# Hybrid decoder trunk on one core: longer load times in the planner's count, the MLP weight sums moved from GpSimd to VectorE, and earlier adding loads for the second MLP product

## The chip, the cores and the metric

The kernel runs on one core of a Trainium2 chip. The metric is the device time of one execution in microseconds (us). TensorE (PE) does the matrix products, VectorE (DVE) and ScalarE (ACT) the elementwise work, GpSimd (POOL) a few sums and the adding loads, and SyncE (SP) issues nearly all DMA transfers.

## The reference

Two decoder layers over x of 1024 tokens by 1024 channels, all in float32. Each layer has a mixer and an MLP, each behind an RMS norm whose output is scaled and shifted by vectors computed from a conditioning vector c.

```python
c_act = silu(c)
for layer in range(2):
    mod = c_act @ ada_w[layer] + ada_b[layer]          # 6 vectors of 1024
    h = rmsnorm(x) * (1 + sc_m) + sh_m
    y = even_mixer(h) if layer == 0 else odd_mixer(h)  # recurrences, retention, gated delta rule
    x = x + gt_m * y
    h = rmsnorm(x) * (1 + sc_f) + sh_f
    x = x + gt_f * (square(relu(h @ w1)) @ w2)         # w1 1024 x 4096, w2 4096 x 1024
out = rmsnorm(x)
```

## The kernel before

**Products in three parts.** A float32 operand is split into a rounded high part (one ACT instruction) and a remainder (one DVE subtraction), and each product is three matmuls of 128x128 by 128x512: high by high, high by low, low by high. The splits of weights go to tiles named `w` (6 slots), those of activations to the general pool `heap` (73 slots of 128x512).

**The MLPs.** Both MLP products use a Winograd form with 7 block products instead of 8. It needs sums of weight blocks. For the first product ("up", `up_factor`) a step s brings two rows of weights in two tiles `raw` (4 slots) and a tile `pad` (4 slots). A block sum x = a21 + a22 is made by an adding load: SP loads a21, then GpSimd issues a DMA that adds a22 on top (`dma_add`). Two more sums are made by an elementwise addition on GpSimd (`G.tensor_tensor`): x + a11 ahead of kind P6, and P2 + x ahead of kind P3. There are 16 steps of 7 kinds in each layer, 112 items of 12 matmuls each. The results go to the DRAM buffer `h_spill`, 7 tiles a step.

The second product ("down", `down_factor`, the last loop of `mlp`) has two groups of 8 steps; a group runs through the kinds P1 P2 P6 P7 P4 P5 P3 with 8 items of 12 matmuls each, 56 items a group and 112 in all. Item n loads its activations six items ahead (`load_h`). The five weight blocks of a step come by `load_block`, at item numbers relative to the group's first item that `W_LOADS` lists: `a11` from 8 items before the group, `a12` from item 0, `x` at 1, 3, ... 15, `a21` at 10, 12, ... 24, and `a22` from 24. `x` and `a21` are a load on SP with an adding load behind it on GpSimd. Two sums per step are made on GpSimd: a11 + x ahead of P6 (items 16 to 23) and a12 + a11 ahead of P7 (items 24 to 31). When the eight items of a kind are done, DVE drains four PSUM banks; after P1 and P6 the drained values go to tiles `blk` (`shared`), and P2 goes on accumulating in the banks of P1. `X_LOADS` brings the residual x back from `x_spill`. `last_adds` adds `shared` to it in the last group.

**The modulation vectors.** A column of `mod` costs one load of 128x1024 into a `raw` tile and one multiply-and-sum on DVE (`ada_unit`). Most are made beside the first mixer; the last 16 of layer 1 are made in the down product of layer 0, one at every item n with n % 4 == 2.

**The order.** Nothing is ordered by hand. Every instruction is recorded with an estimated duration, and `place()` plays the program through once at build time: of the instructions whose inputs it counts as ready, each engine takes the one of highest priority. The order that comes out is fixed for each engine and each DMA issuer, and the engines run it strictly in that order. A load counts as landed by

```python
dma_free = max(dma_free, now) + op.bytes / 380.0
op.end = dma_free + 2000.0
```

in nanoseconds, adding loads with twice their bytes. Weight work has the highest priority (`bias(-2 * BIG)`), the drains come next, and the matmuls follow program order.

Of the kernel before, what the change touches and what calls it, by code (L numbers as in the profile page):

```python
# [16 lines left out]
ALU = mybir.AluOpType  # L17
# [140 lines left out]
class Recorder:  # L158
# [59 lines left out]
    def place(self):  # L218
        free = {p: list(range(t.n)) for p, t in self.pools.items()}
        front = {}  # L220
        for p, d in self.unplaced.items():
            front[p] = sorted(d)
        for op in self.ops:
            op.npred, op.ready, op.start = len(op.preds), 0.0, None
            for p in op.preds:
                p.succ.append(op)
        queue = {p: deque(self.fifo[p]) for p in FIFO}
        waiting = {e: [] for e in ENGINES}
        avail = {e: [] for e in ENGINES}
        engine_free = {e: 0.0 for e in ENGINES}  # L230
        dma_free = port_free = 0.0
        events = [(0.0, 0, 0)]
        frees = []
        tick = 0
        for op in self.ops:
            if not op.npred:
                heapq.heappush(waiting[op.eng], (0.0, op.prio, op.seq))
        order = []

        def placeable(op, now):  # L240
            need = {}
            for b in op.bufs:
                if b.busy > now:
                    return False
                if b.pool is not None and b.slot is None:
                    need[b.pool] = need.get(b.pool, 0) + 1
            for b in op.bufs:
                if b.pool in FIFO and b.slot is None and b is not queue[b.pool][0]:
                    return False
            for p, n in need.items():  # L250
                lead = front[p]
                while lead and not self.unplaced[p][lead[0]]:
                    lead.pop(0)
                keep = 0 if op.group <= lead[0] else self.reserve.get(p, 0)
                if len(free[p]) < n + keep:
                    return False
            return True

        while len(order) < len(self.ops):
            if not events:  # L260
                raise RuntimeError("no instruction can be placed")
            now = events[0][0]
            while events and events[0][0] <= now:
                heapq.heappop(events)
            while frees and frees[0][0] <= now:
                _, _, b = heapq.heappop(frees)
                free[b.pool].append(b.slot)
            for e in ENGINES:
                w = waiting[e]
                while w and w[0][0] <= now:  # L270
                    _, prio, seq = heapq.heappop(w)
                    heapq.heappush(avail[e], (prio, seq))
                if engine_free[e] > now:
                    continue
                skipped = []
                chosen = None
                while avail[e]:
                    item = heapq.heappop(avail[e])
                    op = self.ops[item[1]]
                    if placeable(op, now):  # L280
                        chosen = op
                        break
                    skipped.append(item)
                for item in skipped:
                    heapq.heappush(avail[e], item)
                if chosen is None:
                    if w:
                        heapq.heappush(events, (w[0][0], tick, 0))
                        tick += 1
                    continue  # L290
                op = chosen
                for b in op.bufs:
                    if b.pool is not None and b.slot is None:
                        b.slot = free[b.pool].pop(0)
                        self.unplaced[b.pool][b.group] -= 1
                        if b.pool in FIFO:
                            queue[b.pool].popleft()
                op.start = max(now, port_free) if op.port else now
                engine_free[e] = op.start + op.dur
                if op.port:  # L300
                    port_free = engine_free[e]
                if e in ("DVE", "ACT"):
                    for b in op.bufs:
                        if b.pool in ("psum", "dps"):
                            b.busy = engine_free[e]
                if op.bytes:
                    dma_free = max(dma_free, now) + op.bytes / 380.0
                    op.end = dma_free + 2000.0
                else:
                    op.end = engine_free[e]  # L310
                heapq.heappush(events, (engine_free[e], tick, 0))
                tick += 1
                order.append(op)
                for s in op.succ:
                    kind = s.preds[op]
                    t = op.start if kind is None else op.end + LATENCY.get((op.eng, s.eng), 150)
                    s.ready = max(s.ready, t)
                    s.npred -= 1
                    if not s.npred:
                        heapq.heappush(waiting[s.eng], (s.ready, s.prio, s.seq))  # L320
                        heapq.heappush(events, (max(s.ready, now), tick, 0))
                        tick += 1
                for b in op.bufs:
                    b.left -= 1
                    b.last = max(getattr(b, "last", 0.0), op.end)
                    if not b.left and b.pool is not None:
                        heapq.heappush(frees, (b.last, tick, b))
                        heapq.heappush(events, (max(b.last, now), tick, 0))
                        tick += 1
        self.order = order  # L330
        return max(op.end for op in order)
# [77 lines left out]
class Tensor:  # L409
# [17 lines left out]
    def transpose(self, o, i, ident):  # L427
# [14 lines left out]
PN = {k: n for n, k in enumerate(UP_ORDER)}  # L442

X_LOADS = {i + n * m: (f, k + m) for i, n, f, k in ((2, 2, 0, 0), (23, 2, 1, 4), (32, 1, 0, 4), (40, 1, 1, 0)) for m in range(4)}
W_LOADS = {(i + n * j, name): j for i, n, name in ((-8, 1, "a11"), (0, 1, "a12"), (1, 2, "x"), (10, 2, "a21"), (24, 1, "a22"))
           for j in range(GRP)}

AHEAD = 4
# [7 lines left out]
def trunk_kernel(ctx, tc, xT, pos, ada0, ada, cols, hsc, lw_a, lw_x, w_ev, w_evo, w_od, w_odg,  # L456
# [142 lines left out]
    def split(dst_hi, dst_lo, src, after=(), eng=V):  # L599
        act(dst_hi, src, AF.Copy, after)  # L600
        eng.tensor_tensor(dst_lo, src, dst_hi.bitcast(F32), ALU.subtract)


    units = []
    loads = {}
# [33 lines left out]
    def up_factor(l, s, kind, pw):  # L639

        a11, a12 = w_1[l, 2 * s][:, 0:HT], w_1[l, 2 * s][:, HT:D]
        a21, a22 = w_1[l, 2 * s + 1][:, 0:HT], w_1[l, 2 * s + 1][:, HT:D]

        def load():

            r = rec.tile("raw")
            dma(r, w_1[l, 2 * s])
            pw["P1"], pw["P2"] = r[:, 0:HT], r[:, HT:D]
            pw["x"] = padded()[:, 0:HT]
            dma(pw["x"], a21)  # L650
            dma_add(pw["x"], a22)
            r = rec.tile("raw")
            dma(r, w_1[l, 2 * s + 1])
            pw["P7"], pw["P4"] = r[:, 0:HT], r[:, HT:D]
            dma_add(pw["P7"], a11)

        def get():
            if s < AHEAD and kind in ("P1", "P2"):
                r = rec.tile("raw")[:, 0:HT]
                dma(r, a11 if kind == "P1" else a12)  # L660
                return factor(r)
            if kind == "P6":
                G.tensor_tensor(pw["x"], pw["x"], pw["P1"], ALU.add)
            if kind == "P3":
                G.tensor_tensor(pw["P2"], pw["P2"], pw["x"], ALU.add)
                return factor(pw["P2"], True)
            return factor(pw["x"] if kind in ("P5", "P6") else pw[kind])
        get.load = load
        return get

    def down_factor(pw, kind):

        def get():
            if kind == "P6":
                G.tensor_tensor(pw["a11"], pw["a11"], pw["x"], ALU.add)
            if kind == "P7":
                G.tensor_tensor(pw["a12"], pw["a12"], pw["a11"], ALU.add)
            n = {"P1": "a11", "P2": "a12", "P5": "x", "P6": "a11", "P7": "a21", "P3": "a12", "P4": "a22"}[kind]
            return factor(pw[n], kind == "P3")
        return get  # L680
# [45 lines left out]
            units.append(w_odo[j])  # L726
    mlp_units(1)

    last_mm = [None]

    def mm3(ps, whi, wlo, kcs, hhi, hlo):
        n = len(kcs)
# [153 lines left out]
    def mlp(l, xh):  # L886
# [113 lines left out]
                                   ALU.mult, ALU.add)  # L1000

        def last_adds(f, ks):
            for k in ks:
                add_to(f, k, shared[k % 4], f == 1 and k < 4)

        for n, (s, k) in enumerate(mlp_plan()):
            up(s, k)
# [7 lines left out]
        for n, (g, kind, j) in enumerate(todo):  # L1015
            if j == 0:
# [3 lines left out]
                    pss = [pmt() for _ in range(4)]  # L1020
                elif first:
                    pss = [pdt(), pdt(), pdt(), pmt()]
            if l == 0 and n % 4 == 2:
                ada_some(1, [marks[-1]])
            whi, wlo = pop()
            bhi, blo = operand(loaded.pop(n))
# [903 lines left out]
```

## Time and profile before

| what | before |
| --- | --- |
| median of 3 runs | 2349.3 us (2345.51 to 2351.92) |
| the profiled execution: time / span | 2352.24 us / 2350.5 us |
| granted TensorE clock, mean | 0.991 |
| busy: PE, DVE, ACT, POOL | 2285.3, 1701.7, 1275.0, 513.5 us |
| moved by DMA | 393.35 MB |

The span is the time from the first to the last instruction. A busy PE counts the instruction as long as it runs, also where the granted clock is lower, so that matmuls in a stretch say more than busy time. The stages by the trace: start to about 75 us, mixer of layer 0 to 325, its output product to about 420, up product to 780, down product to about 1090, mixer of layer 1 to 1625, its output product to 1715, up product to 2030, down product and the final norm to the end.

### The profile page before, as it was taken

Reading aid. Unit: us, or ns where it says so; the run is one execution under the profiler, and the core shown is the slowest. Engines: PE = TensorE matmul, PEld = TensorE weight load, DVE = VectorE, ACT = ScalarE, POOL = GpSimd, SP = SyncE. Lnnn points to the kernel's source line nnn. Section 1 sums busy time; section 2 is a strip of 40 time slices with the busy share of each in tenths; the row PEclk is TensorE's granted clock in tenths of the full one; section 3 lists DMA queues with packets and bytes.
Section 4 is the critical chain, followed back from the end, with each engine's and each line's share of the span. In section 5 each row is a group of like instructions: output and inputs, shape, how many; then the busy total and the mean of one; then the engine's idle time right before and its main releaser. Section 6 shows DMA issues by size and latency. Waiting matters only on the chain.

```text
span 2350.5 us, 31521 instructions
## 1 busy us (share of the span) xinstructions
PE 2285.3 (97%) x10906; PEld 1871.1 (80%) x10906; DVE 1701.7 (72%) x2702; ACT 1275.0 (54%) x2377; POOL 513.5 (22%) x602
## 2 busy tenths in 40 slices
PE   7999999899999999999999999999999999999998
PEld 4787888678878778887787887888878888788886
DVE  7997667896555786887976687566687555676776
ACT  6787453565545544445755574656465555544444
POOL 3000000022221230500073426430022222140500
PEclk9999999999999999999999999999999999999999
DMA  8253338757664997753212122244358665896752
GB/s 290 90 135 117 117 120 283 246 157 219 192 180 156 311 346 244 211 189 117 73 39 77 48 57 68 59 141 141 128 154 238 194 188 159 265 312 193 185 161 94
DMA packets 199076, 393.35 MB, mean 167 GB/s; under 512 B 30146, under 2 KB 40962, under 8 KB 198916
## 3 DMA queue, kind: packets, MB, share of 16 engines
q1 hardware_dynamic: 180484, 357.78, 45.5%
q0 software_dynamic: 18432, 33.56, 8.8%
q8 instruction: 85, 1.39, 0.2%
q14 instruction: 75, 0.61, 0.1%
HBM read 308.91 MB, written 82.35 MB: 166 GB/s over the span
## 4 chain that ended last, share of the span: by engine, by line
PE 73%; issue 7%; DMA 7%; DVE 6%; ACT 5%; POOL 1%; SPq 0%; POOLq 0%; DVEq 0%; ACTq 0%
PE dps L342 39%; PE psum L342 35%; ACT heap L342 4%; DVE heap L342 4%; DMA raw<-in_dram 3%; DMA heap<-in_dram 1%; DMA h_spill<-heap 1%; DVE w L342 1%; ACT w L342 1%; POOL pad L342 1%; DVE raw L342 1%; DMA heap<-h_spill 1%; POOL raw L342 0%; POOL heap L342 0%; ACT L342 0%
## 5 line engine op out<-in xcount | busy, mean ns | idle before, releaser
L342 PE MATMUL dps<-heap,w 128*128 128x512 f32 x5016 | 1246.2, 396 | 14.9 <-DVE heap L342 8.7
L342 PEld LDWEIGHTS dps<-heap,w 128*128 128x128 f32 x5016 | 928.0, 189 | 211.0 <-ACT heap L342 10.6
L342 PE MATMUL psum<-heap,w 128*128 128x512 f32 x3816 | 899.7, 392 | 14.7 <-DVE blk L342 5.8
L342 PEld LDWEIGHTS psum<-heap,w 128*128 128x128 f32 x3816 | 718.9, 189 | 173.2 <-ACT heap L342 10.1
L342 ACT ACTIVATE heap<-heap 128x512 f32<-128x512 f32 (+2 forms) x1055 | 619.9, 609 | 258.6 <-DVE heap L342 200.5
L342 DVE TENSOR_TENSOR heap<-heap,heap 128x512 f32<-128x512 f32 (+1 forms) x799 | 580.2, 750 | 79.9 <-ACT heap L342 75.1
L342 ACT ACTIVATE w<-heap 128x512 fp32r<-128x512 f32 x224 | 140.6, 630 | 276.3 <-PE psum L342 219.9
L342 ACT ACTIVATE w<-raw 128x512 fp32r<-128x512 f32 (+1 forms) x248 | 192.2, 778 | 175.0 <-PE dps L342 93.6
L342 DVE TENSOR_TENSOR w<-raw,w 128x512 fp32r<-128x512 f32 (+1 forms) x213 | 192.9, 910 | 75.1 <-ACT w L342 69.6
L342 DVE TENSOR_TENSOR w<-heap,w 128x512 fp32r<-128x512 f32 x192 | 159.5, 836 | 97.1 <-ACT w L342 96.6
L342 POOL DMA_DIRECT2D raw<-in_dram x32 | 27.9, 873 | 718.5 <-DMA x_spill<-heap 297.3
L342 POOL TENSOR_TENSOR blk<-blk,blk 32x31 f32<-32x31 f32 (+15 forms) x248 | 173.9, 701 | 38.6 <-DMA blk<-n_full 11.5
L342 POOL TENSOR_TENSOR heap<-heap,heap 128x512 f32<-128x512 f32 x74 | 114.4, 1557 | 201.6 <-ACT heap L342 103.5
L342 ACT ACTIVATE heap<-psum 128x512 f32<-128x512 f32 (+6 forms) x189 | 89.3, 480 | 81.3 <-PE psum L342 80.4
L342 PE MATMUL psum<-heap,heap 128*128 128x128 f32 (+4 forms) x1064 | 130.5, 264 | 2.5 <-DVE heap L342 2.2
L342 PEld LDWEIGHTS psum<-heap,heap 128*128 128x128 f32 (+2 forms) x1064 | 113.1, 169 | 23.6 <-DVE heap L342 5.0
L342 DVE SCALAR_TENSOR_TENSOR raw<-raw,blk 128x1024 f32<-128x1024 f32 x80 | 98.8, 1237 | 30.2 <-DMA raw<-in_dram 29.8
L342 POOL DMA_DIRECT2D heap<-in_dram x64 | 59.8, 979 | 268.9 <-DVE heap L342 137.4
L342 DVE TENSOR_TENSOR w<-pad,w 128x512 fp32r<-128x512 f32 x64 | 58.3, 910 | 75.3 <-ACT w L342 75.2
L342 ACT ACTIVATE w<-pad 128x512 fp32r<-128x512 f32 x64 | 40.4, 632 | 126.0 <-POOL pad L342 71.4
L342 DVE TENSOR_TENSOR heap<-psum,heap 128x512 f32<-128x512 f32 x89 | 61.0, 686 | 48.2 <-PE psum L342 39.5
L342 ACT ACTIVATE heap<-dps 128x512 f32<-128x512 f32 (+1 forms) x134 | 77.5, 585 | 24.0 <-PE dps L342 13.7
(180 smaller groups left out, 1384.8 us busy)
## 6 DMA issues: line engine op xcount, KB each, us to landing
raw<-in_dram SPq DMA_DIRECT2D x232, 512.0 KB, 4.1
heap<-in_dram SPq DMA_DIRECT2D x226, 256.0 KB, 5.6
h_spill<-heap SPq DMA_DIRECT2D x224, 256.0 KB, 4.4
heap<-h_spill SPq DMA_DIRECT2D x224, 256.0 KB, 5.2
heap<-in_dram POOLq DMA_DIRECT2D x64, 256.0 KB, 6.8
x_spill<-heap SPq DMA_DIRECT2D x48, 256.0 KB, 3.1
heap<-x_spill SPq DMA_DIRECT2D x48, 256.0 KB, 5.4
pad<-in_dram SPq DMA_DIRECT2D x32, 256.0 KB, 2.5
```

What stands on the lines that cost most here:

```text
L342: op.call(*a, **k)
```

## The change

The planner counts 360 instead of 380 bytes a nanosecond and 3.5 us (SP) or 5.5 us (GpSimd) instead of 2.0 us behind a load. The four kinds of weight sums go to DVE. In the down product `x` is loaded from 7 items before the group instead of item 1, `a12` from -1 instead of 0, `a21` from 4 instead of 10, `a22` from 22 instead of 24. The modulation columns in the down product of layer 0 start at item 34 and come every 3 items. `last_adds` gets a lower priority. `last_mm` is defined earlier in the file, which moves no instruction.

```diff
-                    dma_free = max(dma_free, now) + op.bytes / 380.0
-                    op.end = dma_free + 2000.0
+                    dma_free = max(dma_free, now) + op.bytes / 360.0
+                    op.end = dma_free + (5500.0 if e == "POOL" else 3500.0)
...
-W_LOADS = {(i + n * j, name): j for i, n, name in ((-8, 1, "a11"), (0, 1, "a12"), (1, 2, "x"), (10, 2, "a21"), (24, 1, "a22"))
+W_LOADS = {(i + n * j, name): j for i, n, name in ((-8, 1, "a11"), (-7, 2, "x"), (-1, 1, "a12"), (4, 2, "a21"), (22, 1, "a22"))
            for j in range(GRP)}
...
             if kind == "P6":
-                G.tensor_tensor(pw["x"], pw["x"], pw["P1"], ALU.add)
+                V.tensor_tensor(pw["x"], pw["x"], pw["P1"], ALU.add)
             if kind == "P3":
-                G.tensor_tensor(pw["P2"], pw["P2"], pw["x"], ALU.add)
+                V.tensor_tensor(pw["P2"], pw["P2"], pw["x"], ALU.add)
...
             if kind == "P6":
-                G.tensor_tensor(pw["a11"], pw["a11"], pw["x"], ALU.add)
+                V.tensor_tensor(pw["a11"], pw["a11"], pw["x"], ALU.add)
             if kind == "P7":
-                G.tensor_tensor(pw["a12"], pw["a12"], pw["a11"], ALU.add)
+                V.tensor_tensor(pw["a12"], pw["a12"], pw["a11"], ALU.add)
...
         def last_adds(f, ks):
-            for k in ks:
-                add_to(f, k, shared[k % 4], f == 1 and k < 4)
+            with bias(LATER):
+                for k in ks:
+                    add_to(f, k, shared[k % 4], f == 1 and k < 4)
...
-            if l == 0 and n % 4 == 2:
+            if l == 0 and n >= 32 and n % 3 == 1:
                 ada_some(1, [marks[-1]])
```

More of the change, by code (lines that the diff above doesn't have):

```diff
@@ L601, in split @@
         eng.tensor_tensor(dst_lo, src, dst_hi.bitcast(F32), ALU.subtract)
+    last_mm = [None]
     units = []
@@ L727, in trunk_kernel @@
     mlp_units(1)
-    last_mm = [None]
     def mm3(ps, whi, wlo, kcs, hhi, hlo):
```

## The prediction

> **What bounds the kernel now.** I read the page first: busy times, DMA queues, the chain that ended last.
>
> ```profile
> PE 2285.3 (97%) x10906; PEld 1871.1 (80%) x10906; DVE 1701.7 (72%) x2702; ACT 1275.0 (54%) x2377; POOL 513.5 (22%) x602
> ...
> q1 hardware_dynamic: 180484, 357.78, 45.5%
> q0 software_dynamic: 18432, 33.56, 8.8%
> ...
> PE 73%; issue 7%; DMA 7%; DVE 6%; ACT 5%; POOL 1%; SPq 0%; POOLq 0%; DVEq 0%; ACTq 0%
> ```
>
> TensorE is the bound: all others together can give back little more than its idle 65 us. So I looked for where matmuls are missing. The next view is the table of stretches (length; busy time and count of PE, PEld, DVE, ACT, POOL; granted clock; DMA share; GB/s), and from the chain a run of twelve matmuls in a quiet stretch.
>
> ```profile
> 400.00:425.00 25.00, 17.56 (x70) 14.06 (x69) 19.38 (x28) 7.32 (x10) 0.00 (x0) 0.86 0.87 283
> 425.00:550.00 125.00, 119.52 (x505) 95.78 (x504) 108.69 (x160) 75.83 (x130) 24.44 (x21) 0.97 0.69 204
> 550.00:775.00 225.00, 222.94 (x980) 183.18 (x979) 127.79 (x189) 115.22 (x202) 44.92 (x40) 1.00 0.61 181
> 800.00:850.00 50.00, 44.50 (x181) 35.77 (x180) 47.18 (x49) 19.32 (x33) 32.47 (x29) 0.93 1.07 329
> 875.00:1050.00 175.00, 174.83 (x771) 144.33 (x770) 136.29 (x198) 76.17 (x134) 36.58 (x32) 1.00 0.70 220
> 1715.00:1800.00 85.00, 80.98 (x350) 64.65 (x349) 75.60 (x110) 57.16 (x101) 25.11 (x21) 1.00 0.67 190
> 1800.00:2025.00 225.00, 224.14 (x987) 184.76 (x986) 129.12 (x190) 116.33 (x204) 44.37 (x39) 1.00 0.62 185
> 2025.00:2075.00 50.00, 47.26 (x202) 38.66 (x201) 40.35 (x45) 21.57 (x37) 25.25 (x22) 0.97 1.04 331
> ```
>
> ```profile
> 548.44 2.72 PE dps L342 x12
> ```
>
> A matmul takes 2.72/12 = 0.2267 us at full pace, an item 2.72 us. Length minus count times 0.2267 is what a stretch loses, idle time and slow clock together: 9.1 at 400 (end of the first output product), 10.5 at 425 and 5.7 at 1715 (starts of the up products), 2.8 and 1.3 in their remainders, 9.0 at 800 and 4.2 at 2025 (starts of the down products), 0.2 at 875, where the second group of layer 0 begins. Together 42.8 us: all that the change can reach. Now the stalls behind it (last bracket: idle time before, and its releaser).
>
> ```profile
> 804.83 23.68 PE L342 MATMUL psum<-heap,w 128*128 128x512 f32 x96 [2.88 <-DVE blk L342]
> ...
> 839.57 3.64 PE L342 MATMUL dps<-heap,w 128*128 128x512 f32 x8 [2.61 <-DVE heap L342]
> ...
> 2050.25 23.63 PE L342 MATMUL psum<-heap,w 128*128 128x512 f32 x96 [2.74 <-DVE blk L342]
> ```
>
> Both down products stall at the same place: P2 may not overwrite the banks of P1 before DVE has drained them (`blk`). The 2.61 is DVE itself being late.
>
> **The change: sums to DVE.** The groups of the whole run, and one moment of the timeline:
>
> ```profile
> L342 POOL TENSOR_TENSOR heap<-heap,heap 128x512 f32<-128x512 f32 x74 | 114.4, 1557 | 201.6 <-ACT heap L342 103.5 <-DMA heap<-in_dram 43.3 <-DVE w L342 34.6
> ...
> L342 DVE SCALAR_TENSOR_TENSOR raw<-raw,blk 128x1024 f32<-128x1024 f32 x80 | 98.8, 1237 | 30.2 <-DMA raw<-in_dram 29.8
> ...
> L342 DVE TENSOR_TENSOR w<-raw,w 128x512 fp32r<-128x512 f32 x128 | 87.1, 689 | 34.4 <-ACT w L342 34.3
> ...
> L342 POOL TENSOR_TENSOR pad<-pad,raw 128x512 f32<-128x512 f32 x32 | 54.0, 1689 | 41.9 <-DVE w L342 41.9
> ...
> L342 POOL TENSOR_TENSOR raw<-raw,pad 128x512 f32<-128x512 f32 x32 | 44.6, 1392 | 7.8 <-DVE w L342 5.9
> ```
>
> ```profile
> 812.71 2.83 POOL L342 TENSOR_TENSOR heap<-heap,heap 128x512 f32<-128x512 f32 x2
> ...
> 812.87 3.24 DVE L342 TENSOR_TENSOR w<-heap,w 128x512 fp32r<-128x512 f32 x1 [0.44 <-ACT w L342]
> ```
>
> ```profile
> L342 DVE TENSOR_TENSOR heap<-heap,heap 128x512 fp32r<-128x512 f32 x16 | 21.2, 1352 | 0.6 <-ACT heap L342 0.6
> L342 DVE TENSOR_TENSOR w<-heap,w 128x512 fp32r<-128x512 f32 x16 | 17.0, 1078 | 4.0 <-ACT w L342 4.0
> ```
>
> 128 sums leave POOL: 64 x 1.557 + 54.0 + 44.6 = 198 us. On DVE each costs 0.689 (same shape, undisturbed), 88 us in all. A DVE subtraction that starts beside two POOL sums takes 3.24 instead of 0.69: it stands until they are done. How much comes back is bounded by 0 and 198 us; nearest are the last two rows, of 800 to 850: 16 x (1.352 - 0.689) + 16 x (1.078 - 0.689) = 16.8 us beside 15 sums (29 POOL instructions in that stretch less its 14 adding loads, whose row stands further down), 1.1 us a sum. So DVE gains about 0.4 us a sum where it is crowded and pays up to 0.69 where it is not. The price on the path, stage by stage:
>
> ```profile
> 487.99 2.87 POOL pad L342
> ...
> 526.62 0.87 POOL raw L342
> 527.49 1.32 POOL pad L342
> ...
> 528.88 1.30 POOL raw L342
> ```
>
> ```profile
> ACT w L342 <- POOL pad L342: 71.4, 23, 4.7
> ```
>
> Starts of the up products, where DVE is busy 108.69 of 125 us: the chain goes through three sums, 5.49 us, which become 3 x 0.689 = 2.07. The other sums there cost and return about the same. -3 of the 10.5; in proportion -1.6 of the 5.7 in layer 1 (bounds: none, and all). Remainders of the up products: ACT stood 71.4 us for POOL sums, with the drains of the banks queued behind it in order; afterwards POOL holds adding loads alone, which no longer stand behind sums in its queue either, and the sum runs on DVE right behind the subtraction that it follows. Two thirds of 2.8 + 1.3: -2.7 (bounds 0 and -4.1).
>
> **Earlier loads, later modulation columns.** By the page's queues a 256 KB load takes 45.5% of 2350.5 us over 357.78 MB, 0.784 us of all 16 DMA engines, and one of the 128 adding loads 8.8% / 128 = 1.62 us. Eight items last 21.8 us, sixteen 43.5.
>
> Layer 0, items 0 to 15 before: a12 8, x 8, a21 3, activations 16, residual 4, late spills 4, modulation 4 double ones: 51 loads and 11 adds, 57.8 us, 14.3 over. After: -8 to -1 take a11 8, a12 1, x 4, activations 6, spills 8, and 4 adds, 27.7, 5.9 over; 0 to 15 take 41 loads and 10 adds, 48.3, 4.8 over: 10.7 behind instead of 14.3. Layer 1, without modulation, goes from 8.0 to 10.7. The second group of layer 0 goes the other way, since the 16 columns, made at items 2 to 62 before, now come at items 34 to 79. Before, items 56 to 71 hold 39 loads and 11 adds, 48.4 us, 4.9 over, with nothing left over from ahead. After, items 48 to 55 hold 27 loads and 4 adds (27.7 us, 5.9 over) and items 56 to 71 hold 43 and 10 (49.9, 6.4 over): 12.3 behind.
>
> ```profile
> heap<-h_spill SPq DMA_DIRECT2D x20, 256.0 KB, 9.0
> ...
> heap<-in_dram POOLq DMA_DIRECT2D x14, 256.0 KB, 7.0
> ```
>
> These are issues from 800 to 850 with their time to landing. Behind the moved loads in SP's queue stand the activation loads. They are issued six items, 16.3 us, ahead and take 9.0 here: 7.3 us of slack, which cover the 5.9 but not all of the 10.7 or 12.3.
>
> Start of down in layer 0 (9.0): DVE's 47.18 us lose 16.8 of waiting and five modulation multiplies (1.24 each) and gain 15 x 0.689: 34.5. Of the 9.0, 2.88 and 2.61 are the stalls and 3.5 the slow clock that goes with them. The 2.61 should go, with half of the clock: -4.4. The first stall hangs on the order before the drain; half of it and its clock, -1.6 more: -6 (bounds -9 and 0). Second group: +2 (0 to +9, the price of the first now). Layer 1 (4.2): DVE had room (40.35 of 50), DMA gets a little worse, the order before the drain better: -2 (bounds -4.2 and +4). Heap tiles are held longer by x, but at item -8 three kinds' operands of the up product, 24 tiles, are already free: 0.
>
> **The longer count.** The planner counted 256 KB as 0.69 + 2.0 us, where the activation loads above took 9.0. Its effect at the end of the first output product, from the waits of 395 to 440:
>
> ```profile
> DVE raw L342 <- DMA raw<-in_dram: 10.7, 10, 1.9
> ...
> PE psum L342 <- ACT heap L342: 7.4, 1, 7.4
> ```
>
> DVE stands ten times for modulation loads that the planner thought landed, and the norm's sums, queued behind, hold PE for 7.4 us. Counting 1.5 us more per load moves the multiplies behind the sums. -2 of the 9.1 (bounds -9 and +2, since the loads themselves fill the queue at a share of 0.87). Everywhere else the order is redrawn too: 0, bounds 4 us either way, about the largest single stall in a mixer:
>
> ```profile
> 1248.41 0.50 PE L342 MATMUL dps<-heap,w 128*128 128x512 f32 x1 [3.52 <-DVE heap L342]
> ```
>
> The Trainium skill ("DMA: Bandwidth & Descriptors", on the two cost components) puts the fixed cost of a DMA at about 2.0 us: by it the old count was right and this part gains nothing, a sum 2 us smaller. The trace disagrees: 9.0 us in the stretch that matters.
>
> **Last adds** in the last group fall back by 300 instructions, about 17 items or 46 us, and have 24 items until the end: 0.
>
> **Sum.** -3 - 1.6 - 2.7 - 6 + 2 - 2 - 2 = -15.3 us against the profiled execution's 2352.24, which is 2337. The median of the runs is 2.9 lower, so 2334.
>
> **Rivals.** *A, DMA stays the limit,* and the earlier loads only move its queue. The backlogs of 10.7 and 12.3 us exceed the slack of 7.3, and the starts of the down products keep their losses: without -6 and -2, sum about -5 with a second group that loses 4 rather than 2: about 2344, no change that shows. For it: DMA share 1.07 and 1.04. Against: the stalls end on DVE, not on a load. *B, slower: DVE inherits POOL's waits for loads.* POOL's sums at the starts of the two down products, from 780 to 875 and from 2020 to 2100:
>
> ```profile
> L342 POOL TENSOR_TENSOR heap<-heap,heap 128x512 f32<-128x512 f32 x16 | 25.0, 1605 | 9.6 <-DMA heap<-in_dram 9.5
> ...
> L342 POOL TENSOR_TENSOR heap<-heap,heap 128x512 f32<-128x512 f32 x16 | 24.8, 1549 | 16.6 <-DMA heap<-in_dram 16.4
> ```
>
> These two alone are 25.9 us that POOL stood for landings. A sum has top priority, so DVE takes it as soon as it is counted as landed; if the load is later, the drains and splits queue behind it, and PE waits for them. At full price 2334 + 26 = 2360. It decides once landings come later than the new count (0.8 + 1.5 + 5.5 = 7.8 us from issue) by more than the lead of DVE. Against: 7.0 measured, now with a shorter backlog in layer 0. *C, more.* The right count also clears the starts of the up products and the 7.4: -15 - 15 = 2319.
>
> **Numbers.** Forecast 0.54, A 0.21, B 0.13, C 0.12. A run tells 0.3% (7 us) from no change: faster is below 2342, slower above 2356. Faster 0.66 (forecast but for its edge, C, a fifth of A), same 0.23, slower 0.11. The forecast's own range is 2326 to 2343; 2322 to 2356 leaves out most of B and half of C.
>
> **What would show it.** POOL busy near 315 us, DVE near its 1700; no wait of ACT for POOL; the 16 and 16 splits from 800 to 850 near 0.69; no 2.61 stall; PE's count there up by some 25 of 181. Wrong: DVE standing for adding loads at items -2 to 13 of a group (B), new PE stalls from 930 to 1020 (the second group), or the `blk` stalls unchanged (A).

## The result and the profile after

| | before | after |
| --- | --- | --- |
| median | 2350.6 us (2345.5 to 2355.4) | 2311.5 us (2308.2 to 2314.1) |
| the profiled execution: time / span | 2352.24 / 2350.5 us | 2310.03 / 2308.3 us |
| after over before | | 0.9831, 95% interval 0.9809 to 0.9854 |

The change saves 39 us, two and a half times what was forecast, and the time lies below the range. The page after:

```profile
PE 2272.8 (98%) x10906; PEld 1868.4 (81%) x10906; DVE 1698.1 (74%) x2830; ACT 1278.1 (55%) x2377; POOL 330.7 (14%) x474
...
q1 hardware_dynamic: 180484, 357.78, 46.1%
q0 software_dynamic: 18432, 33.56, 9.0%
...
PE 81%; issue 6%; DVE 5%; ACT 5%; DMA 3%; SPq 0%; POOL 0%; POOLq 0%; DVEq 0%; ACTq 0%
```

The work is the same: as many matmuls, as many bytes, and DVE as busy as before although it has 128 more instructions. TensorE's idle time (span less busy time) fell from 65.2 to 35.5 us, 30 us, and its busy time by 12.5 us: the granted clock was 0.86, 0.97, 0.93 and 0.97 in four of the stretches with stalls and is 1.00 there now. The stretches that the prediction showed, moved to where their stages lie now (length; busy time and count of PE, PEld, DVE, ACT, POOL; granted clock; DMA share; GB/s):

```profile
400.00:425.00 25.00, 25.00 (x112) 20.68 (x111) 22.41 (x34) 10.53 (x14) 0.00 (x0) 1.00 0.96 342
425.00:550.00 125.00, 123.81 (x542) 100.79 (x541) 113.13 (x181) 81.76 (x144) 11.12 (x13) 1.00 0.73 220
550.00:770.00 220.00, 220.00 (x973) 182.21 (x972) 139.21 (x216) 117.69 (x201) 17.57 (x21) 1.00 0.65 198
775.00:825.00 50.00, 49.57 (x219) 40.70 (x218) 37.10 (x60) 23.01 (x40) 9.58 (x11) 1.00 1.08 339
850.00:1025.00 175.00, 174.55 (x770) 143.87 (x769) 140.91 (x229) 78.54 (x137) 13.91 (x16) 1.00 0.74 230
1690.00:1790.00 100.00, 99.83 (x441) 82.35 (x440) 86.58 (x140) 66.99 (x118) 10.42 (x12) 1.00 0.72 213
1790.00:2000.00 210.00, 210.00 (x928) 173.91 (x927) 134.14 (x206) 112.26 (x191) 16.55 (x19) 1.00 0.64 193
2000.00:2050.00 50.00, 49.81 (x220) 40.86 (x220) 36.57 (x58) 22.48 (x39) 10.44 (x12) 1.00 1.08 336
```

At 0.2267 us a matmul nearly all of the 42.8 us of loss is gone (about 3 are left, 2.1 of them from 425 to 550): 112 matmuls instead of 70 at 400, 219 and 220 instead of 181 and 202 in the first 50 us of the down products. And the DMA engines are as full at the down products as before: 1.08 and 1.08, where they were at 1.07 and 1.04. Two more views show what went with the losses, the groups of DVE from 775 to 825 and the waits of ACT and DVE for DMA over the whole run:

```profile
L342 DVE TENSOR_TENSOR heap<-heap,heap 128x512 fp32r<-128x512 f32 x20 | 13.5, 683 | 1.3 <-ACT heap L342 1.3
L342 DVE TENSOR_TENSOR w<-heap,w 128x512 fp32r<-128x512 f32 x18 | 12.4, 689 | 12.6 <-ACT w L342 12.6
```

```profile
ACT heap L342 <- DMA heap<-h_spill: 7.8, 10, 1.7
...
DVE raw L342 <- DMA raw<-in_dram: 4.7, 6, 2.6
```

The splits take 0.68 and 0.69 us where they took 1.35 and 1.08. Over the run ACT stood 38.9 us and DVE 29.8 us for these two kinds of loads before.

### The profile page after: what moved, and what is told of

It reads as the page before. It is cut to its first block, busy times and chain, and to the rows that moved or that the text cites. A ratio compares the mean times of both kernels' runs of the same rounds, so it can differ in the third digit from the quotient of the medians.

```text
span 2308.3 us, 31439 instructions
## 1 busy us (share of the span) xinstructions
PE 2272.8 (98%) x10906; PEld 1868.4 (81%) x10906; DVE 1698.1 (74%) x2830; ACT 1278.1 (55%) x2377; POOL 330.7 (14%) x474
## 4 chain that ended last, share of the span: by engine, by line
PE 81%; issue 6%; DVE 5%; ACT 5%; DMA 3%; SPq 0%; POOL 0%; POOLq 0%; DVEq 0%; ACTq 0%
PE psum L342 41%; PE dps L342 40%; ACT heap L342 3%; DVE heap L342 3%; DMA raw<-in_dram 1%; DMA heap<-in_dram 1%; DVE w L342 1%; ACT w L342 1%; DMA heap<-h_spill 1%; DVE raw L342 1%; SPq L342 0%; DMA h_spill<-heap 0%; ACT L342 0%; ACT pad L342 0%; POOL heap L342 0%
## 5 line engine op out<-in xcount | busy, mean ns | idle before, releaser
L342 PE MATMUL psum<-heap,w 128*128 128x512 f32 x3816 | 890.5, 389 | 2.3 <-DVE heap L342 1.8
L342 DVE TENSOR_TENSOR w<-heap,w 128x512 fp32r<-128x512 f32 x192 | 132.3, 689 | 120.0 <-ACT w L342 119.6
L342 DVE SCALAR_TENSOR_TENSOR heap<-pad,col,heap 128x512 f32<-128x512 f32 x96 | 78.3, 819 | 0.3
L342 DVE TENSOR_TENSOR w<-pad,w 128x512 fp32r<-128x512 f32 x64 | 44.1, 690 | 39.3 <-ACT w L342 39.2
```

The lines of the kernel that those rows point to most:

```text
L342: op.call(*a, **k)
```

## The experiments

Two theories were set against each other. *The count*: engines stood in front of loads that the planner thought landed, with drains and norm sums queued behind. *The sums*: sums on GpSimd hold up DVE and, behind it, the drains. A third was the prediction's own for the down products: DMA supply at their start.

### The three parts, alone and together

| count | sums on DVE | load and modulation items | median | over before, 95% interval |
| --- | --- | --- | --- | --- |
| old | no | old | 2350 to 2352 us | 1 |
| new | no | old | 2349.2 | 0.9987 (0.9969 to 1.0005) |
| old | yes | old | 2328.2 | 0.9895 (0.9874 to 0.9916) |
| old | no | new | 2362.2 | 1.0044 (1.0027 to 1.0062) |
| new | yes | old | 2317.4 | 0.9850 (0.9824 to 0.9875) |
| old | yes | new | 2331.7 | 0.9920 (0.9905 to 0.9934) |
| new | no | new | 2343.1 | 0.9964 (0.9951 to 0.9978) |
| new | yes | new | 2311.5 | 0.9831 (0.9809 to 0.9854) |

The rows are, in order, the kernel before and six kernels that each take some of the change's hunks as they stand, then the changed kernel; the lower priority of the last adds goes with the new items in the last three rows, is missing where the new items stand alone, and was not tried apart. What was expected of them, in the same order:

```diff
# count alone
-                    dma_free = max(dma_free, now) + op.bytes / 380.0
-                    op.end = dma_free + 2000.0
+                    dma_free = max(dma_free, now) + op.bytes / 360.0
+                    op.end = dma_free + (5500.0 if e == "POOL" else 3500.0)
# sums alone (four places)
-                G.tensor_tensor(...)
+                V.tensor_tensor(...)
# items alone: W_LOADS and the condition on ada_some of the change
```

> The kernel before with the planner's longer count alone. Theory 1 (the count did most: instructions were queued in front of drains and norm sums for loads that had not landed): 2320 to 2330 us; the 7.4 us stall at the end of the first output product and the blk stalls of 2.9 and 2.7 us gone; the 2.6 us stall that ended on DVE stays. Theory 2 (the sums on GpSimd did most, by the port that DVE shares with it and by ACT waiting for them): 2340 to 2350 us. Theory 3 (less DMA work at the starts of the down products did most): about 2345, with the stalls at 800 still there.

> The kernel before with the 128 sums on DVE alone, the old count. Theory 1: 2340 to 2350 us or slower, since DVE now takes sums for adding loads that are counted as landed after 3.4 us and land after 6.8. Theory 2: 2325 to 2335 us, the starts of the up products down from 10.5 and 5.7 us of loss to half, no ACT waits for POOL. Theory 3: about 2345.

> The kernel before with the new load items and modulation items alone. Theory 1 and 2: 2345 to 2352 us, the stalls keep their places. Theory 3: 2335 to 2342 us, the losses of 9.0 and 4.2 us at the starts of the down products gone.

> Count and sums together, old load and modulation items. If the two parts carry the whole gain: 2311 to 2316 us. Theory 3, or a need for all parts: 2322 us or more, with the loss left at the starts of the down products.

> The changed kernel with the old load count. With the sums alone the kernel took 2328 us, with the new load items alone 2362. If the loads cost because the sums on GpSimd then run in bursts, the new items are harmless once the sums are on DVE: 2322 to 2330 us, with the 7.4 us stall of the first output product back. If the new items overload the DMA queue by themselves: 2335 to 2345 us.

> The changed kernel with the sums left on GpSimd. If the sums on GpSimd are the main cause of the losses in the MLPs: 2340 to 2360 us, with DVE subtractions of 3 to 6 us beside runs of GpSimd sums and stalls that end on drains. If count and loads carry the gain: 2315 to 2325.

The sums carry the most: 22 us alone, 31 to 32 beside either or both of the other parts. The count is worth nothing by itself (its interval holds 1), 11 us once the sums are on DVE, 20 beside all else. The new items make the kernel slower while the sums are on GpSimd and the count is old (12 us), and save 6 when both others are there (the intervals of these two rows overlap). Two results lie outside what was expected: nobody expected the new items alone to come out slower, at 2362 us, and all but the count came out at 2331.7, between its two ranges. Every row also has an order of its own, since the planner draws it anew, so that a few us between two rows need a place in the traces before they have a cause.

The parts do not add up, and the kernels that gained nothing show why. The count alone does remove the stall of 7.44 us near 420 and both `blk` stalls: up to 850 us it has done 53 matmuls more than the kernel before. It then loses them again: it is 31 ahead at 1050, 22 at 2090 and 13 behind at 2250. The timeline of the count alone shows the largest of the new stalls, 5.44 us in the second down product (start; length; engine; the last bracket is the idle time before and its releaser):

```profile
2196.46 4.42 DVE L342 TENSOR_TENSOR heap<-heap,heap 128x512 fp32r<-128x512 f32 x1
2196.55 1.61 POOL L342 TENSOR_TENSOR heap<-heap,heap 128x512 f32<-128x512 f32 x1
...
2197.79 1.22 POOL L342 DMA_DIRECT2D heap<-in_dram  x1
2198.40 1.92 POOL L342 TENSOR_TENSOR heap<-heap,heap 128x512 f32<-128x512 f32 x1
...
2200.41 3.26 POOL L342 TENSOR_TENSOR heap<-heap,heap 128x512 f32<-128x512 f32 x2
2200.80 3.42 DVE L342 TENSOR_TENSOR w<-heap,w 128x512 fp32r<-128x512 f32 x1
...
2204.14 2.47 DVE L342 TENSOR_TENSOR blk<-blk,psum 128x512 f32<-128x512 f32 x4
2204.38 1.43 POOL L342 TENSOR_TENSOR heap<-heap,heap 128x512 f32<-128x512 f32 x1
2204.96 2.47 PE L342 MATMUL psum<-heap,w 128*128 128x512 f32 x5 [5.44 <-DVE blk L342]
```

Two subtractions of 0.69 us take 4.42 and 3.42. GpSimd works off a row of sums meanwhile, with gaps of 0.24 us and less; each subtraction stands through at least two of them and ends about half a us after one of them does. The four drains that TensorE waits for stand behind them. The kernel with the new items alone has the same at the start of its first down product, with one subtraction of 5.57 us:

```profile
799.53 5.57 DVE L342 TENSOR_TENSOR w<-heap,w 128x512 fp32r<-128x512 f32 x1
799.62 2.77 POOL L342 TENSOR_TENSOR heap<-heap,heap 128x512 f32<-128x512 f32 x2
...
802.07 1.18 POOL L342 DMA_DIRECT2D heap<-in_dram  x1
...
802.67 1.87 POOL L342 TENSOR_TENSOR heap<-heap,heap 128x512 f32<-128x512 f32 x1
...
805.85 2.47 PE L342 MATMUL psum<-heap,w 128*128 128x512 f32 x5 [5.15 <-DVE blk L342]
```

In both the row of sums lies just ahead of a drain. That is how one can place loads better and lose.

### Is it the port or the waiting for results?

GpSimd's sums could cost by what waits for them, or by what they take from DVE while they run. So in the changed kernel, where nothing waits for GpSimd's sums any more, GpSimd got idle work beside each of the 128 DVE sums: once a product of the whole sum tile with itself, once a short product and two fills.

```diff
+    def beside(t):
+        d = ht("dmy")
+        G.tensor_tensor(d, t, t, ALU.mult)
# the other kernel, in place of the last line
+        G.tensor_tensor(d[:, 0:8], t[:, 0:8], t[:, 0:8], ALU.mult)
+        G.memset(d, 0.0)
+        G.memset(d, 0.0)
...
                 V.tensor_tensor(pw["x"], pw["x"], pw["P1"], ALU.add)
+                beside(pw["x"])
```

> The changed kernel, and behind each of the 128 DVE sums GpSimd squares the sum into a scratch tile that nobody reads. Nothing waits for GpSimd, so only the port that DVE and GpSimd share, and the release of the tiles, are left. Theory A (sums on GpSimd cost by holding DVE's second input): 2325 us or more, 10 to 25 us of the gain gone, DVE splits in the MLPs at 0.8 to 1.3 us instead of 0.69. Theory B (they cost since ACT and the adding loads wait for GpSimd's results): 2309 to 2315 us.

> As the one before, but the GpSimd work beside each sum is a product of 8 columns and two fills of the scratch tile, about as long in all, and almost none of it reads SBUF. Theory A: 2309 to 2316 us, splits at 0.69 to 0.75. If GpSimd's time in front of the adding loads is what counts: like the one before.

The products cost 58 us (2369.1, ratio to before 1.0081, 1.0064 to 1.0098), the fills 2, which is not clear of noise (2313.3, 0.9839, 0.9825 to 0.9854). The busy times, first with the products, then with the fills:

```profile
PE 2294.0 (97%) x10906; PEld 1877.2 (79%) x10906; DVE 1751.3 (74%) x2830; ACT 1279.4 (54%) x2377; POOL 489.9 (21%) x602
```

```profile
PE 2274.1 (98%) x10906; PEld 1869.8 (81%) x10906; DVE 1698.5 (73%) x2830; ACT 1278.5 (55%) x2377; POOL 530.8 (23%) x858
```

GpSimd is busier with the fills, and DVE's same 2830 instructions take 53 us longer with the products. Waiting for GpSimd is small in both: ACT, DVE and TensorE wait 5.0 us in all with the products and 7.3 with the fills, SP's queue 29.8 and 35.5. Two differences are left: the products read and the fills hardly do, and the sum tile is held for a shorter product with the fills, which these waits do not show to matter. So GpSimd's reading, through the port that it shares with DVE, is enough to cost this much. That nothing else costs in the sums themselves does not follow. With the sums on GpSimd and the rest of the change, ACT waits 18.9 us in all for GpSimd's results (98.2 in the kernel before), and that may be part of the 32.

My number for the splits was off: over the whole run they average 0.715 and 0.766 us with the products (0.716 and 0.781 from 770 to 1050, in a down product), less than the 0.787 and 0.836 of the kernel before, which is 18 us faster. In part that is because DVE has the 128 sums on top here: it is busy 1751.3 us, before 1701.7. And the mean stretch does not tell the price, which hangs on what is queued behind the stretched instruction. From the timeline with the products, where three sums of 0.69 us take 2.73 ahead of a drain:

```profile
2213.30 2.73 DVE L342 TENSOR_TENSOR heap<-heap,heap 128x512 f32<-128x512 f32 x3
2214.14 3.79 POOL L342 TENSOR_TENSOR heap<-heap 128x512 f32<-128x512 f32 x3 [0.47 <-DVE heap L342]
2215.95 2.47 DVE L342 TENSOR_TENSOR blk<-blk,psum 128x512 f32<-128x512 f32 x4
2216.78 2.47 PE L342 MATMUL psum<-heap,w 128*128 128x512 f32 x5 [5.44 <-DVE blk L342]
```

The Trainium skill ("SBUF — State Buffer", § Who interferes with whom) says that a DVE instruction with two SBUF inputs contends with a GpSimd instruction that reads SBUF, and not with one that only writes it. The pair of runs agrees: 58 us where GpSimd reads, 2 where it mostly fills.

### Up or down product

```diff
# up products: the two sums of up_factor; down products: the two of down_factor
-                V.tensor_tensor(...)
+                G.tensor_tensor(...)
```

> The changed kernel with the 64 sums of the up products back on GpSimd. All 128 back cost 31.6 us. If the price is DVE's and in proportion to the sums: 2325 to 2330 us. If it sits at the starts of the up products, where DVE has least room: 2320 to 2326, with the loss at 475 to 550 and 1700 to 1800 back and none at the down products.

> The changed kernel with the 64 sums of the down products back on GpSimd. In proportion: 2325 to 2330 us, with stalls at drains 8 to 32 items into a group and DVE subtractions of 3 us and more. If only the up products matter: 2311 to 2316.

2324.6 us (0.9891, 0.9871 to 0.9911) and 2330.8 (0.9918, 0.9904 to 0.9933): 13 and 19 us, which add up to the 32 of all. The up products' two starts, with their sums on GpSimd:

```profile
425.00:550.00 125.00, 120.26 (x522) 96.97 (x521) 109.80 (x163) 78.80 (x138) 28.78 (x24) 1.00 0.74 215
1690.00:1790.00 100.00, 98.19 (x413) 78.38 (x412) 82.42 (x122) 63.67 (x113) 28.82 (x24) 0.97 0.69 194
```

The changed kernel has 542 and 441 matmuls there, so that 4.5 and 6.3 us are lost at 0.2267; behind the starts nothing is (972 and 928 matmuls from 550 to 770 and 1790 to 2000, where it has 973 and 928). The port is not shown to be the only cause here: ACT waits 11.2 us for these sums. The place is as the second of the two readings had it. The down sums show at 770 to 850 (334 of 351) and in the second group, 850 to 1050 (848 of 879), the latter with a 4.58 us stall on `blk`, and in layer 1 from 2000 to 2090 (385 of 396) and 2090 to 2200 (473 of 487).

### What the count does

The changed kernel without the new count stalls for 3.28 and 4.99 us at the first drain of its two down products although the sums are off GpSimd. The later stall, on ACT, DVE and PE, and the end of the same drain in the changed kernel:

```profile
2025.47 0.63 ACT L342 ACTIVATE heap<-heap 128x512 fp32r<-128x512 f32 x1 [4.07 <-DMA heap<-h_spill]
...
2026.13 0.69 DVE L342 TENSOR_TENSOR heap<-heap,heap 128x512 fp32r<-128x512 f32 x1 [3.20 <-ACT heap L342]
...
2027.94 0.68 DVE L342 TENSOR_SCALAR blk<-psum 128x512 f32<-128x512 f32 x1
...
2028.78 1.62 PE L342 MATMUL psum<-heap,w 128*128 128x512 f32 x3 [4.99 <-DVE blk L342]
```

```profile
2010.70 13.54 PE L342 MATMUL psum<-heap,w 128*128 128x512 f32 x59
2010.90 0.68 DVE L342 TENSOR_SCALAR blk<-psum 128x512 f32<-128x512 f32 x1
...
2011.50 0.68 DVE L342 TENSOR_TENSOR heap<-heap,heap 128x512 fp32r<-128x512 f32 x1
...
2011.55 0.63 ACT L342 ACTIVATE heap<-heap 128x512 fp32r<-128x512 f32 x1 [0.47 <-DMA heap<-h_spill]
```

The remainder of an activation that had not landed was queued ahead of the drain. With the new count the drain comes first, and TensorE runs on, while the loads take about as long: the seven activation loads issued from 2015 to 2035 without the new count land after 7.0 us (median), the seven from 1997 to 2017 in the changed kernel after 6.7. Counted in matmuls, the old count loses 34 at 395 to 425, 19 at 770 to 850 and 30 at 2000 to 2090: 18.8 of its 20 us. Which loads must be counted longer?

```diff
# 512 KB loads alone
+                    op.end = dma_free + (3500.0 if e == "SP" and op.bytes == 4 * P * D else 2000.0)
# SP's 256 KB transfers alone (with 360 bytes a nanosecond)
+                    op.end = dma_free + (3500.0 if e == "SP" and op.bytes == 4 * P * HT else 2000.0)
# longer than the change
+                    op.end = dma_free + (7500.0 if e == "POOL" else 5000.0)
```

> The changed kernel, in which the planner counts the longer time only for the 512 KB loads into raw tiles (weights of the mixers and up products, modulation columns) and the old 2.0 us and 380 bytes a nanosecond for all others. The count is worth 20.2 us there. If its price sits in the order of modulation loads and norm sums at the end of the first output product: 2318 to 2323 us, the 7.7 us stall near 420 gone and the rest left. If all of it sits there: 2311 to 2315. If it sits in the activation loads and adding loads: 2326 to 2332.

> The changed kernel, in which the planner counts 3.5 us only for SP's 256 KB transfers (activations, plain weight blocks, residual, spills) and 2.0 us for the 512 KB loads and for the adding loads on GpSimd. With none of it counted longer 2331.7 us, with the 512 KB loads alone 2328.4, with all 2311.5. If the drains stood behind splits of activations that had not landed: 2312 to 2318 us, and no stalls at drains near 790 and 2025. If DVE stood for adding loads instead: 2322 to 2330.

> The changed kernel with 5.0 us counted on SP and 7.5 us on GpSimd. The activation loads land 6.4 us after issue at the starts of the down products, so that a longer count should not hurt: 2306 to 2313 us. If a count past the usual 4 to 5 us puts work too late elsewhere: 2316 to 2325.

The 512 KB loads alone give 2328.4 us (0.9907, 0.9892 to 0.9922), little better than the old count; the stall near 420 goes from 6.01 to 3.22 us and not away. The 256 KB transfers alone give 2333.4 (0.9927, 0.9905 to 0.9948), no better than the old count and slower than either of the ranges expected. The waits of each, over the whole run:

```profile
ACT heap L342 <- DMA heap<-h_spill: 36.4, 23, 3.8
...
DVE raw L342 <- DMA raw<-in_dram: 13.6, 8, 4.5
```

```profile
DVE raw L342 <- DMA raw<-in_dram: 29.3, 26, 4.2
...
ACT heap L342 <- DMA heap<-h_spill: 18.3, 17, 2.2
```

Without the new count the two waits are 34.6 and 24.4 us. Each kernel about halves its own kind and leaves the other. The first still stands 3.69 and 5.59 us at the drains; the second loses those two stalls, as expected, but has 3.17 and 3.42 us at the norm's sums (420 and 469) and 2.06 us at 2056. Neither kind is enough alone; whether the adding loads must be counted longer too was not tried apart.

The longer count gives 2333.8 us (0.9926, 0.9911 to 0.9942) and refutes "a longer count should not hurt": the starts of the down products stay clean (no stall of 0.4 us or more from 770 to 850), but the second group of layer 0 and the mixer of layer 1 get worse, and the time lies above both ranges expected. That mixer in the changed kernel; then the second group and the mixer with the longer count:

```profile
1050.00:1690.00 640.00, 633.37 (x3524) 525.94 (x3523) 448.37 (x751) 370.84 (x730) 197.74 (x327) 0.99 0.29 87
```

```profile
850.00:1050.00 200.00, 195.49 (x851) 159.69 (x851) 156.79 (x254) 90.51 (x157) 15.05 (x20) 0.99 0.68 213
1050.00:1690.00 640.00, 625.45 (x3460) 518.41 (x3459) 444.50 (x750) 367.10 (x727) 196.53 (x326) 0.99 0.28 84
```

TensorE is idle 14.6 us in the mixer instead of 6.6, and in the second group 28 matmuls behind (851 for 879, 6.3 us). Whether that is the count being too long for the mixer's short loads or only one more redrawn order is not settled by these runs.

### Load items and modulation items

```diff
# old modulation items in the changed kernel
-            if l == 0 and n >= 32 and n % 3 == 1:
+            if l == 0 and n % 4 == 2:
# old weight items in the changed kernel: W_LOADS as before
```

> The changed kernel with the old items for the modulation loads. New load items and modulation items together are worth 5.9 us beside the other parts. If DMA supply at the first group of layer 0 is what they relieve: 2314 to 2318 us, with a new stall between 780 and 850. If supply does not matter: 2309 to 2314.

> The changed kernel with the old items for a12, x, a21 and a22; the modulation loads stay at item 34 and later. With both old 2317 us, with new weight items and old modulation items 2320, with both new 2311.5. If the modulation items alone carry the gain: 2308 to 2312 us. If the early adding loads need them but add something: 2313 to 2316.

2319.7 us (0.9874, 0.9857 to 0.9891) and 2316.5 (0.9846, 0.9828 to 0.9865). The later modulation loads are worth 8 us beside the new weight items, and without them stalls of 1.37 and 2.27 us stand at 804 and 812. The new weight items are worth 5 us beside the late modulation loads, not clear of noise (the intervals overlap), and none beside the old ones (2317.4 with both old). So supply in the first group does bind, but for a few us and only when the two collide; neither kind of item alone gave a measurable gain.

## Why the prediction was wrong

The stalls were found, most of their causes named, and the direction was right. The sizes were not; the forecast was -15.3 us and the change brings -39.

- **Sums on DVE, the step that failed most.** I priced DVE's wait as an average, 1.1 us per sum, set the DVE time that the sums cost against it, and came to -3 and -1.6 at the up products and -2.7 behind; in the down products the gain stood within the -6 and -2. Putting the sums back costs 32 us. At the starts of the up products the balance of DVE time ("the other sums there cost and return about the same") was the step that failed: the sums alone, with everything else as before, give 541 matmuls instead of 505 from 425 to 550 and 440 instead of 416 from 1690 to 1790, 8.2 and 5.4 us. The average was the wrong measure in the down products too: one subtraction beside a row of sums takes 4.42 or 5.57 us, and the drains of a whole kind queue behind it. The timeline of before showed the short form, 3.24 us beside two sums, and I took it for two sums' worth. In the up products the longest found before the change is 4.12 us for two subtractions, at 511; which wait makes up the loss there was not taken apart.
- **The remainders of the up products, put at -2.7.** Their loss went, but the step was wrong. ACT's 71.4 us of waiting for GpSimd's sums went with late loads: GpSimd itself stood 57.0 us for loads into `pad`. With the count alone, the sums still on GpSimd, ACT's wait falls to 4.9 us, and the remainders run 972 and 928 matmuls from 550 to 770 and 1790 to 2000 instead of 958 and 921, as many as after the change but for one. The sums alone clear them as well.
- **The count, put at -2.** It is worth 20 us beside the other parts and about nothing alone. I saw the 7.4 us stall but took a fifth of its loss, on the ground that the loads fill the DMA queue; the stall went entirely while the share rose from 0.87 to 0.96. (The 9.0 us that I set against the planner's 2.7 are the time to landing in the fullest stretch; over the run before the median of these loads is 5.2.) The first drain stalls, of which I took half for the order ahead of the drain, are the count's doing too, once GpSimd's sums are gone. The -1.6 for that half also does not come out of its own terms: half of 2.88 is 1.4, and half of the clock left to it (1.75) is 0.9, 2.3 together; this moves the sum by 0.7 us.
- **DMA supply.** The sum of loads and adds gave backlogs of 10.7 to 12.3 us and +2 us for the second group. The new order runs through the second group without a loss (174.55 of 175 us busy) and through the starts of the down products at a DMA share of 1.08. Rival A is refuted: the losses went although the queue stayed full, once the drains were not queued behind late loads any more. Its small true part is the 8 us of the modulation loads.
- **Rival B**, DVE inheriting GpSimd's waits, hardly occurred: with the sums alone and the old count DVE stood 6.4 us for adding loads, where 26 were feared, and in the changed kernel no such wait shows among its largest.
- **Rival C** had the right mechanism and 0.12 of the chance; even it stopped 8 us short, since it left the down products with half of their losses.
- **The marks.** DVE near 1700: 1698.1. POOL near 315: 330.7. No ACT wait for POOL in the MLPs, splits at 0.69, no 2.61 stall: all so. Matmuls in the 50 us around the start of the down product: 38 more, not 25.

By stage, the forecast fell short by 7 us at the end of the first output product, 9.5 at the starts of the up products, 5 at the starts of the down products, 1.4 in the remainders and 2 in the second group. The prediction treated causes as terms of a sum. The table shows that they cover for each other: the parts alone give 1, 22 and -12 us, all together 39.

## What to carry to other kernels

When an in-order engine has an urgent short job now and then, such as a drain, price what may stand in front of it at its worst and not on average; look for the longest single instruction of a group, not at its mean. Work on GpSimd that reads SBUF is not free while DVE does additions and subtractions of two SBUF tiles, even if nobody waits for its result. An engine named as releaser may itself have stood for a load: follow the wait one step further before it is priced. A planner's wrong latency shows only where something urgent is queued behind the late load, and parts of a change that remove two causes of the same stall must be tried together before either is called useless.

## What was not expected of the hardware

A DVE subtraction with two SBUF inputs can stand through several GpSimd instructions in a row: 5.57 us instead of 0.69, across three sums with an adding-load issue between them. GpSimd work of about the same length that mostly fills cost 2 us where reading work cost 58, and DVE's busy time did not rise with 128 more instructions (1701.7 before, 1698.1 after).
